# Input projection of a hybrid decoder layer: parts of A's queries and keys written two tiles late, weight loads moved up, inputs kept by token tile, bias rows stored one by one, attention B's loads moved up

## The chip, the cores and the metric

The kernel runs on one core of one Trainium2 chip. The metric is the device time of one execution in microseconds. The core's engines are TensorE (PE), VectorE (DVE), ScalarE (ACT), GpSimd (POOL) and SyncE (SP); each works through its own instructions in order. All data moves between memory and the on-chip buffers through DMA engines that the core's queues share.

## The reference

One decoder layer in float32, 2048 tokens of width 1024. Two head groups, A (sliding window, 8 query heads and 2 key heads, rotary positions) and B (8 heads, three dilated branches with a relative-position bias), read one normalised input through one projection.

```
h = rmsnorm(x, g_attn)
proj = einsum('bsd,de->bse', h, w_in) + b_in        # w_in: 1024 x 2304
qa, ka, va, qb, kb, vb = split(proj)                # 512, 128, 128, 512, 512, 512
oa = sliding_window_sink_gqa(rope(qa), rope(ka), va, sinks)
ob = dilated_mixture(qb, kb, vb, rel_table)         # branches (128,1), (512,4), (2048,16)
mixed = concat(rmsnorm(oa, g_out_a), rmsnorm(ob, g_out_b))
x = x + mixed @ w_o
h = rmsnorm(x, g_ffn)
x = x + (silu(h @ w_gate) * (h @ w_up)) @ w_down
return rmsnorm(x, g_final)
```

## The kernel before

Every float32 operand of a matrix product is kept as two parts, a high part in a reduced format and the rest, and a product is three matmuls: high by high, rest by high, high by rest. The kernel runs in stages: the input is normalised and transposed, and the values of both groups are projected (to about 146 us of the profiled execution); A's keys and queries are projected and rotated (146 to 270); B's queries and keys are projected while A's attention runs (280 to 576); then attention B, the output projection and the feed-forward layer, which takes the second half of the span.

A scheduler in the tile framework sets the order of the instructions on each engine. It takes the program's order and its own estimate of durations; a tile's buffers are taken in turn from a pool with a fixed number of them (`bufs`), and whoever writes into a buffer waits for its last reader.

The names that matter here, all in `project`, `bias_tables` and `attend_b`:

- `hh` and `hl` hold the two parts of the normalised input, 128 partitions by 8 chunks of the width by 2048 tokens. Tokens come in four tiles of 512. `gemm` (L173) makes one output block of 128 columns by one token tile with 24 matmuls into a PSUM buffer `acc`.
- `load_w` (L161 to L165) loads a block of the weights (`raw`) and splits it (`wh` on ScalarE, `wl` on VectorE).
- A's loop goes over the column blocks c = 4 (the keys), 0, 1, 2, 3, and inside over the token tiles. `acc` is copied with its quarters exchanged into `t1` (L298 on ScalarE, L300 on VectorE), multiplied by the rotary tables (L302, L303), summed on GpSimd into `t2` (L304), and split into the two parts of `hia` (the cast L308 on ScalarE, the subtraction L309 on VectorE). `hia` holds all four token tiles of a block and has one buffer. After the fourth tile `store_heads` (L179) writes it to `qA` or `kA` in memory, two DMAs of 1 MB.
- `bias_tables` makes one table per head of B. `rows` multiplies on TensorE (`accb`, L381), copies three rows on ScalarE into `lt` (L382) and stores them to `Ls` (L383). `table` loads pieces of them (L387, L389, L392) into `tt`, `n4` and `n1`, which have one buffer each, rearranges them on VectorE (L393, L394) and stores the table to `Ts` (L396). The steps of the eight heads are laid between the tiles of A's loop.
- `proj_b` makes B's queries and keys, 32 units of one block and token tile, with the parts in `hi` (L331, L332), stored to `qB` and `kB` by `store_heads` on SyncE. `MixerA` (A's attention) runs between the units; its loads of A's keys are at L529.
- `attend_b` loads for each head q (L604), k (L609), the bias table (L612) and v (L621 to L627), all on SyncE. The logits are at L429, the products with v at L494.

Of the kernel before, what the change touches and what calls it, by code (L numbers as in the profile page):

```python
# [10 lines left out]
F32 = mybir.dt.float32  # L11
# [10 lines left out]
NH = 8  # L22
# [125 lines left out]
def project(tc, es, ident, half, x, g_attn, w_in, b_in, sinks, rel, rope, mask_a, onehot, sc):  # L148
# [3 lines left out]
    cp = es.enter_context(tc.tile_pool(name="c1", bufs=1, reuse_waits="tile"))  # L152
    gcol = cp.tile([P, KC], F32, name="gcol")
    bcol = cp.tile([P, 18], F32, name="bcol")
    hh = cp.tile([P, KC, S], F32R, name="hh")
    hl = cp.tile([P, KC, S], F32R, name="hl")
    wr = es.enter_context(tc.tile_pool(name="w1", bufs=2, reuse_waits="tile"))

    def load_w(c0):
# [8 lines left out]
    def gemm(ps, w, t, tag="mm"):  # L168
        acc = ps.tile([P, 512], F32, tag=tag, name="acc")
        n = 0  # L170
        for k in range(KC):
            for a, h in ((w[0], hh), (w[0], hl), (w[1], hh)):
                nc.tensor.matmul(acc, a[:, k, :], h[:, k, t * 512:(t + 1) * 512], start=(n == 0), stop=(n == 3 * KC - 1))  # L173
                n += 1
        return acc

    def store_heads(dst, h, hi, cols):
        for u in range(2):
            nc.sync.dma_start(dst[h + u].rearrange("s d n -> d s n")[:, :, cols], hi[u * 64:u * 64 + 64].bitcast(F32))  # L179


    with ExitStack() as ex:
# [22 lines left out]
        def norm_x(t):  # L205
# [20 lines left out]
            for k in range(KC):  # L226
                pt = ps.tile([P, 512], F32, tag="mm", name="pt")
                for i in range(4):
                    nc.tensor.transpose(pt[:, i * P:(i + 1) * P], ht[i][:, k * P:(k + 1) * P], ident)
                hs = hh[:, k, t * 512:(t + 1) * 512]  # L230
                nc.scalar.activation(hs, pt, AF.Copy, scale=gcol[:, k:k + 1])
                nc.vector.scalar_tensor_tensor(hl[:, k, t * 512:(t + 1) * 512], pt, gcol[:, k:k + 1],
                                               hs.bitcast(F32), op0=ALU.mult, op1=ALU.subtract)

        def v_rows(w, hf, r):
            acc = ps.tile([P, 320], F32, tag="mm", name="accv")
            n = 0
            for k in range(KC):
                for h, b in ((hh, w[0]), (hh, w[1]), (hl, w[0])):
                    nc.tensor.matmul(acc, h[:, k, r * P:(r + 1) * P], b[:, k, :], start=(n == 0), stop=(n == 3 * KC - 1))  # L240
# [35 lines left out]
    with ExitStack() as ex:  # L276
        ps = ex.enter_context(tc.tile_pool(name="ps2", bufs=8, space=PSUM, reuse_waits="tile"))
        rc = ex.enter_context(tc.tile_pool(name="r2", bufs=1, reuse_waits="tile"))
        tab = rc.tile([P, 2, S], F32, name="tab")
        for t in range(NT):  # L280
            cols = slice(t * 512, (t + 1) * 512)
            nc.sync.dma_start(tab[:, :, cols], rope[:, :, cols].rearrange("s p n -> p s n"))
        bsw = rc.tile([P, 5], F32, name="bsw")
        for q4 in range(4):
            nc.vector.tensor_copy(bsw[q4 * 32:(q4 + 1) * 32, :], bcol[(q4 ^ 1) * 32:((q4 ^ 1) + 1) * 32, 0:5])
        bias = bias_tables(tc, ex, ps, rel, onehot, sc)
        rp = ex.enter_context(tc.tile_pool(name="r1", bufs=2, reuse_waits="tile"))
        for n, c in enumerate((4, 0, 1, 2, 3)):
            w = load_w(c * P)
            hi = rp.tile([P, 2, S], F32R, tag="hi", name="hia", bufs=1)  # L290
            for t in range(NT):
                cols = slice(t * 512, (t + 1) * 512)
                acc = gemm(ps, w, t)
                t1 = rp.tile([P, 512], F32, tag="t1", name="t1")
                for q4 in range(4):
                    d, s4 = t1[q4 * 32:(q4 + 1) * 32, :], acc[(q4 ^ 1) * 32:((q4 ^ 1) + 1) * 32, :]
                    if q4 % 2:
                        nc.scalar.copy(d, s4)  # L298
                    else:
                        nc.vector.tensor_copy(d, s4)  # L300
                t2 = rp.tile([P, 512], F32, tag="t2", name="t2")
                nc.vector.scalar_tensor_tensor(t2, acc, bcol[:, c:c + 1], tab[:, 0, cols], op0=ALU.add, op1=ALU.mult)  # L302
                nc.vector.scalar_tensor_tensor(t1, t1, bsw[:, c:c + 1], tab[:, 1, cols], op0=ALU.add, op1=ALU.mult)  # L303
                nc.gpsimd.tensor_add(t2, t2, t1)  # L304

                hj = [hi[:, u].rearrange("p (j r a) -> p r j a", j=16, r=16)[:, 4 * t:4 * t + 4] for u in range(2)]
                t2 = t2.rearrange("p (r j a) -> p r j a", r=4, j=16)
                nc.scalar.copy(hj[0], t2)  # L308
                nc.vector.tensor_sub(hj[1], t2, hj[0].bitcast(F32))  # L309
                if t == NT - 1:  # L310
                    store_heads(sc.qA if c < 4 else sc.kA, 2 * c if c < 4 else 0, hi, slice(0, S))
                m = n * NT + t - 2
                if 0 <= m < 2 * NH:
                    bias(m // NH, m % NH)


    with ExitStack() as ex:
        ps = ex.enter_context(tc.tile_pool(name="ps3", bufs=2, space=PSUM, reuse_waits="tile"))
        ev = ex.enter_context(tc.tile_pool(name="e3", bufs=2, reuse_waits="tile"))
        att = MixerA(tc, ex, ident, sinks, mask_a, sc)  # L320
        w = None

        def proj_b(todo, ps=ps, tag="mm"):
            nonlocal w
            for c0, c, t in todo:
                if t == 0:
                    w = load_w(c0 + c * P)
                bc = bcol[:, c0 // P + c:c0 // P + c + 1]
                acc = gemm(ps, w, t, tag)
                hi = ev.tile([P, 2, 512], F32R, tag="hi", name="hi")  # L330
                nc.scalar.activation(hi[:, 0], acc, AF.Identity, bias=bc)  # L331
                nc.vector.scalar_tensor_tensor(hi[:, 1], acc, bc, hi[:, 0].bitcast(F32), op0=ALU.add, op1=ALU.subtract)  # L332
# [15 lines left out]
def bias_tables(tc, es, ps, rel, onehot, sc):  # L348
# [13 lines left out]
    ones = bp.tile([P, P], F32, name="ones")  # L362
    nc.vector.memset(ones, 1.0)
    for b in range(3):
        o32 = bw.tile([P, 384], F32, tag="lt", name="o32", bufs=1)
        nc.sync.dma_start(o32, onehot[:, b, :])
        nc.vector.tensor_copy(ohr[:, b, :], o32)

# [6 lines left out]
    def rows(h):  # L375
        lw = bw.tile([P, P], F32R, tag="lw", name="lw")
        nc.vector.tensor_scalar(out=lw, in0=ones, scalar1=rhi[:, h:h + 1].bitcast(F32), scalar2=None, op0=ALU.mult)
        lt = bw.tile([P, 3, 384], F32, tag="lt", name="lt", bufs=1)
        for b in range(3):
            acc = ps.tile([P, 384], F32, tag="mm", name="accb")  # L380
            nc.tensor.matmul(acc, lw, ohr[:, b, :], start=True, stop=True)  # L381
            nc.scalar.copy(lt[:, b, :], acc)  # L382
        nc.sync.dma_start(sc.L[h].rearrange("b p n -> p b n"), lt)  # L383

    def table(h):
        tt = bw.tile([P, 640], F32, tag="tt", name="tt", bufs=1)
# [910 lines left out]
```

## Time and profile before

| | us |
|---|---|
| median of three runs | 2429.14 |
| lowest and highest | 2422.71, 2431.72 |
| profiled execution | 2422.51 |
| span of that execution | 2420.7 |
| TensorE busy in it | 2299.3 (95%) |
| VectorE, ScalarE, GpSimd busy | 1602.5, 1055.3, 466.1 |
| mean granted clock of TensorE | 0.975 |

The span is what the profile covers; 1.8 us of the profiled execution lie around it. In a row of the timeline the first number is the start, the second the length, then engine, line, operation and names, with the number of like instructions behind an x; in brackets stands how long the engine had been idle before, and what ended that. PEld is the loading of weights into TensorE. SPq and ACTq are the DMA issues of SyncE and ScalarE.

### The profile page before, as it was taken

What the parts mean: (1) busy time and instruction counts of PE and PEld (TensorE: products, weight loads), DVE (VectorE), ACT (ScalarE), POOL (GpSimd) and SP (SyncE); (2) the same over time, 40 slices, a digit from 0 to 9 for tenths busy, and PEclk for the clock granted to TensorE, in tenths of its full rate; (3) what the DMA queues carried; (4) which work ended last, traced back from release to release, by engine and by line L of the source; (5) the groups of instructions that cost most, each with busy time, mean ns of one, the idle gap of its engine ahead of it and who ended that gap; (6) DMA issues with size and microseconds to landing.
All of it is one profiled execution on the core that took longest, in us unless ns stands there. A gap on an engine that the chain in (4) does not pass through costs nothing.

```text
span 2420.7 us, 33828 instructions
## 1 busy us (share of the span) xinstructions
PE 2299.3 (95%) x11765; PEld 1957.9 (81%) x11765; DVE 1602.5 (66%) x3151; ACT 1055.3 (44%) x2371; POOL 466.1 (19%) x418
## 2 busy tenths in 40 slices
PE   7998889997999989897999999999999999999998
PEld 7987678886999878776788888778888878888887
DVE  5345544446999977658877776796776746657555
ACT  5323245452988873325323323343323325444442
POOL 2321211111111010014132322423232331000000
PEclk9999999998999989998999999999999999999999
DMA  7657575659798686855645445342332329768651
GB/s 222 208 190 196 135 196 164 177 146 248 197 217 216 169 268 175 260 168 183 204 148 173 157 153 170 115 150 96 101 114 94 111 79 396 264 194 292 200 191 70
DMA packets 279835, 436.20 MB, mean 180 GB/s; under 512 B 23968, under 2 KB 152608, under 8 KB 272880
## 3 DMA queue, kind: packets, MB, share of 16 engines
q1 hardware_dynamic: 275648, 423.41, 57.2%
q0 software_dynamic: 3728, 10.30, 1.5%
q8 instruction: 93, 1.52, 0.3%
q14 instruction: 78, 0.64, 0.1%
q10 hardware_dynamic: 288, 0.33, 0.0%
HBM read 286.50 MB, written 147.46 MB: 179 GB/s over the span
## 4 chain that ended last, share of the span: by engine, by line
PE 51%; DVE 3%; DMA 1%; issue 1%; POOL 0%; ACT 0%; DVEq 0%; POOLq 0%; SPq 0%; ACTq 0%
PE bY L1225 7%; PE Yu L1031 7%; PE Yg L1031 7%; PE bZ L1225 5%; PE bX L1225 5%; PE Xu L1031 5%; PE Zu L1031 5%; PE Xg L1031 4%; PE Zg L1031 4%; PE acco L893 2%; DMA hraw<-hT 1%; DMA ob<-oB 1%; DVE xs L915 0%; DVE wl L998 0%; DVE s L979 0%
## 5 line engine op out<-in xcount | busy, mean ns | idle before, releaser
L1178 DVE TENSOR_TENSOR o<-r,o 128x1024 fp32r<-128x1024 f32 x154 | 190.7, 1244 | 139.2 <-ACT o L1177 132.1
L1177 ACT CAST o<-r 128x1024 fp32r<-128x1024 f32 x154 | 162.2, 1054 | 227.4 <-DMA r<-in_w_down_dram 62.6
L1125 POOL TENSOR_TENSOR c<-c,c 128x512 f32<-128x512 f32 x66 | 104.6, 1585 | 569.9 <-DVE c L1049 373.3
L996 ACT CAST wh<-T 128x512 fp32r<-128x512 f32 x176 | 107.4, 621 | 245.0 <-PE Yu L1031 78.8
L476 DVE TENSOR_TENSOR hl<-pt,hl 128x512 fp32r<-128x512 f32 (+1 forms) x224 | 145.7, 658 | 82.5 <-ACT hl L475 81.9
L451 ACT ACTIVATE p<-t,m 128x256 f32<-128x256 f32 (+1 forms) x384 | 176.7, 476 | 20.0 <-DVE m L676 20.0
L173 PE MATMUL acc<-hh,wh 128*128 128x512 f32 x416 | 166.0, 399 | 16.9 <-DVE t L302 9.6
L1225 PE MATMUL bY<-o 128*128 128x512 f32 x792 | 180.5, 389 | 0.0
L1225 PEld LDWEIGHTS bY<-o 128*128 128x128 f32 x792 | 148.6, 188 | 30.9
L893 PE MATMUL acco<-woh,oT 128*128 128x512 f32 x512 | 165.3, 401 | 4.7 <-ACT oT L864 3.9
L173 PE MATMUL acc<-hh,wl 128*128 128x512 f32 x416 | 165.5, 398 | 0.0
L173 PE MATMUL acc<-hl,wh 128*128 128x512 f32 x416 | 165.0, 397 | 0.0
L998 DVE TENSOR_TENSOR wl<-T,wh 128x512 fp32r<-128x512 f32 x176 | 152.7, 879 | 0.3
L494 PE MATMUL o<-hl,v 128*128 128x128 f32 (+1 forms) x816 | 142.8, 296 | 5.9 <-DVE hl L476 4.9
L475 ACT CAST hl<-pt 128x512 fp32r<-128x512 f32 (+1 forms) x224 | 124.7, 566 | 47.9 <-PE pt L470 47.6
L429 PE MATMUL s<-k,q 128*128 128x256 f32 (+1 forms) x768 | 126.2, 299 | 16.5 <-DMA k<-kB 7.9
L470 PE MATMUL pt<-ident,p 128*128 128x128 f32 x848 | 135.8, 282 | 2.5 <-DVE hl L476 1.5
L429 PEld LDWEIGHTS s<-k,q 128*128 128x128 f32 x768 | 105.2, 201 | 24.2 <-DVE nma L566 7.1
L494 PEld LDWEIGHTS o<-hl,v 128*128 128x128 f32 x816 | 113.0, 195 | 11.1 <-DVE hl L476 8.7
L1225 PE MATMUL bX<-o 128*128 128x512 f32 x528 | 120.6, 389 | 1.1 <-DVE o L1178 1.1
L1225 PE MATMUL bZ<-o 128*128 128x512 f32 x528 | 120.3, 389 | 0.0
L893 PEld LDWEIGHTS acco<-woh,oT 128*128 128x128 f32 x512 | 97.9, 192 | 27.3 <-ACT oT L864 4.5
(465 smaller groups left out, 5804.5 us busy)
## 6 DMA issues: line engine op xcount, KB each, us to landing
r<-actS SPq DMA_DIRECT2D x154, 256.0 KB
actS<-c SPq DMA_DIRECT2D x128, 256.0 KB
wraw_g<-in_w_gate_dram SPq DMA_DIRECT2D x44, 512.0 KB
wraw_u<-in_w_up_dram SPq DMA_DIRECT2D x44, 512.0 KB
r<-wT SPq DMA_DIRECT2D x88, 256.0 KB
r<-in_w_down_dram SPq DMA_DIRECT2D x66, 256.0 KB
k<-kB SPq DMA_DIRECT2D x32, 512.0 KB
draw<-in_w_down_dram SPq DMA_DIRECT2D x22, 512.0 KB
```

The source lines that it names most:

```text
L173: nc.tensor.matmul(acc, a[:, k, :], h[:, k, t * 512:(t + 1) * 512], start=(n == 0), stop=(n == 3 * KC - 1))
L429: nc.tensor.matmul(s[:, i, :n], b["q"], b["k"][m], start=(m == 0), stop=(m == 1))
L451: nc.scalar.activation(b["pv"](p[:, i, :n]), b["tv"](b["t"]), AF.Exp, scale=-1.0, bias=nm[:, c:c + 1], accum_out=l[:, c:c + 1])
L470: nc.tensor.transpose(pt[:, sl, :], p[:, i, hfn * P:(hfn + 1) * P], ident)
L476: nc.vector.tensor_sub(lo, pt[:, a:z, :], hi.bitcast(F32))
L494: nc.tensor.matmul(out, v[:, vi, :], mov, start=(first and n == 1), stop=(last and n == 2 * len(jobs)))
L893: nc.tensor.matmul(acc, oT[kk // 2][:, kk % 2, a, i * P:(i + 1) * P], b[:, kk, :], start=(n == 0), stop=(n == 11))
L998: nc.vector.tensor_sub(lo, src, hi.bitcast(F32))
L1031: nc.tensor.matmul(bank, a[:, k], b[:, k], start=(first and m == 0), stop=(m == 11), skip_group_check=not first)
L1177: nc.scalar.copy(o[:, 0], r)
L1178: V.tensor_sub(o[:, 1], r, o[:, 0].bitcast(F32))
L1225: nc.tensor.matmul(bank[i], o[:, u, 0, i * P:(i + 1) * P], o[:, v, 1, :], start=(first and j == 0 and m == 0), stop=(j == NP - 1 and m == ...
```

## The change

Six edits:

1. The inputs `hh` and `hl` become four tiles each, one per token tile.
2. In A's loop, the split of `t2` into `hia` (now the function `parted`) is written two token tiles after the rest of its tile (`rotated`), and `t2` has four buffers instead of two.
3. The weights of A's next column block are loaded at the second token tile of the current one.
4. In `bias_tables` each row has its own `lt` buffer out of two, and its own store: three DMAs of 192 KB per head instead of one of 576 KB.
5. B's last column block of queries and that of keys are made by turns, token tile by token tile, and their stores are issued by ScalarE.
6. With these, the scheduler places other instructions differently, attention B's first loads among them.

```diff
-    hh = cp.tile([P, KC, S], F32R, name="hh")
-    hl = cp.tile([P, KC, S], F32R, name="hl")
+    hh, hl = [], []
+    for t in range(NT):
+        hh.append(cp.tile([P, KC, 512], F32R, name=f"hh{t}"))
+        hl.append(cp.tile([P, KC, 512], F32R, name=f"hl{t}"))
...
-    def store_heads(dst, h, hi, cols):
+    def store_heads(dst, h, hi, cols, q=nc.sync):
         for u in range(2):
-            nc.sync.dma_start(dst[h + u].rearrange("s d n -> d s n")[:, :, cols], hi[u * 64:u * 64 + 64].bitcast(F32))
+            q.dma_start(dst[h + u].rearrange("s d n -> d s n")[:, :, cols], hi[u * 64:u * 64 + 64].bitcast(F32))
...
+        def rotated(c, t, w):
...
+            t2 = rp.tile([P, 512], F32, tag="t2", name="t2", bufs=4)
...
+            return t2.rearrange("p (r j a) -> p r j a", r=4, j=16)
+
+        def parted(c, t, t2):
+
+            if t == 0:
+                his[c] = rp.tile([P, 2, S], F32R, tag="hi", name="hia", bufs=1)
+            hi = his[c]
...
+            nc.scalar.copy(hj[0], t2)
+            nc.vector.tensor_sub(hj[1], t2, hj[0].bitcast(F32))
+            if t == NT - 1:
+                store_heads(sc.qA if c < 4 else sc.kA, 2 * c if c < 4 else 0, hi, slice(0, S))
+
+        his, behind, w = {}, [], {}
+        seq = [(c, t) for c in (4, 0, 1, 2, 3) for t in range(NT)]
+        w[4] = load_w(4 * P)
+        for n, (c, t) in enumerate(seq):
+            t2 = rotated(c, t, w[c])
+            if t == 1 and n + 3 < len(seq):
+                cn = seq[n + 3][0]
+                w[cn] = load_w(cn * P)
+            behind.append((c, t, t2))
+            if len(behind) > 2:
+                parted(*behind.pop(0))
+            if 0 <= n - 2 < 2 * NH:
+                bias((n - 2) // NH, (n - 2) % NH)
+        for x_ in behind:
+            parted(*x_)
...
-                store_heads(sc.kB if c0 == C_KB else sc.qB, 2 * c, hi, slice(t * 512, (t + 1) * 512))
+                store_heads(sc.kB if c0 == C_KB else sc.qB, 2 * c, hi, slice(t * 512, (t + 1) * 512),
+                            nc.scalar if c == 3 else nc.sync)
...
-        units = [(c0, c, t) for c in range(4) for c0 in (C_QB, C_KB) for t in range(NT)]
+        units = [(c0, c, t) for c in range(3) for c0 in (C_QB, C_KB) for t in range(NT)]
+        units += [(c0, 3, t) for t in range(NT) for c0 in (C_QB, C_KB)]
...
-        o32 = bw.tile([P, 384], F32, tag="lt", name="o32", bufs=1)
+        o32 = bw.tile([P, 384], F32, tag="lt", name="o32")
...
-        lt = bw.tile([P, 3, 384], F32, tag="lt", name="lt", bufs=1)
         for b in range(3):
             acc = ps.tile([P, 384], F32, tag="mm", name="accb")
             nc.tensor.matmul(acc, lw, ohr[:, b, :], start=True, stop=True)
-            nc.scalar.copy(lt[:, b, :], acc)
-        nc.sync.dma_start(sc.L[h].rearrange("b p n -> p b n"), lt)
+            lt = bw.tile([P, 384], F32, tag="lt", name="lt")
+            nc.scalar.copy(lt, acc)
+            nc.sync.dma_start(sc.L[h, b], lt)
```

Three places show what this makes of the order. The rows give line, operation, what is written and read, and the shape; a row with an x stands for so many in a run.

ScalarE around the first casts of the second column block (the pair of `hia` that waits for the store of `kA`), before:

```order
61 L298 COPY t_1879<-acc 32x512 x2
62 L308 CAST hia<-t_1835 128x4x16x8
63 L308 CAST hia<-t_1884 128x4x16x8
64 L298 COPY t_1928<-acc 32x512
65 L382 COPY lt<-accb 128x384 x3
66 L298 COPY t_1928<-acc 32x512
67 L163 CAST wh_2208<-raw_2206 128x1024
68 L298 COPY t_1977<-acc 32x512
69 L382 COPY lt<-accb 128x384
70 L308 CAST hia<-t_1933 128x4x16x8
```

The same place now:

```order
63 L297 COPY t_1890<-acc 32x512 x2
64 L312 CAST hia<-t_1842 128x4x16x8
65 L402 COPY lt<-accb 128x384
66 L312 CAST hia<-t_1895 128x4x16x8
67 L402 COPY lt<-accb 128x384
68 L297 COPY t_1951<-acc 32x512
69 L402 COPY lt<-accb 128x384
70 L297 COPY t_1951<-acc 32x512
71 L402 COPY lt<-accb 128x384 x2
72 L165 CAST wh_2122<-raw_2120 128x1024
73 L312 CAST hia<-t_1956 128x4x16x8
```

The casts stand where they stood; the copies of the bias rows are spread singly between them, each with a store of its own behind it.

ScalarE at the end of A's projection (the last column block; t_2444 and t_2492, now t_2475 and t_2523, are its token tiles 0 and 1), before:

```order
100 L298 COPY t_2487<-acc 32x512 x2
101 L308 CAST hia<-t_2444 128x4x16x8
102 L308 CAST hia<-t_2492 128x4x16x8
103 L298 COPY t_2535<-acc 32x512 x2
104 L163 CAST wh_2963<-raw_2961 128x1024
```

And now:

```order
107 L297 COPY t_2518<-acc 32x512 x2
108 L312 CAST hia<-t_2475 128x4x16x8
109 L312 CAST hia<-t_2523 128x4x16x8
110 L297 COPY t_2568<-acc 32x512 x2
111 L165 CAST wh_3001<-raw_2999 128x1024
```

Nothing moved here: both casts still stand ahead of the copies of token tile 2. On SyncE, the store of the third column block and the tables of the last two heads, before:

```order
161 L396 DMA Ts<-tt 128x640
162 L392 DMA n_2502<-Ls 32x1x256 x4
163 L387 DMA tt<-Ls 128x128
164 L396 DMA Ts<-tt 128x640
165 L179 DMA qA<-hia 64x2x2048 x2
166 L537 DMA qa<-qA 128x2x512 x2
```

And now:

```order
177 L416 DMA Ts<-tt 128x640
178 L412 DMA n_2535<-Ls 32x1x256
179 L181 DMA qA<-hia 64x2x2048 x2
180 L407 DMA tt<-Ls 128x128
181 L412 DMA n_2535<-Ls 32x1x256 x2
182 L416 DMA Ts<-tt 128x640
183 L557 DMA qa<-qA 128x2x512 x2
```

The store now stands ahead of the last head's table, of which the remaining loads and the store of `Ts` follow it. SyncE at the start of attention B, before:

```order
242 L179 DMA kB<-hi 64x2x512 x2
243 L533 DMA va<-vA 128x5x128
244 L179 DMA kB<-hi 64x2x512 x2
245 L604 DMA q_5428<-qB 128x2048
246 L609 DMA k_0_5430<-kB 64x2048 x2
247 L609 DMA k_0_5433<-kB 64x2048 x2
248 L612 DMA tab_5436<-Ts 128x640
249 L627 DMA v_2_5438<-vJ 128x16x128
250 L604 DMA q_5446<-qB 128x2048
```

And now:

```order
256 L553 DMA va<-vA 128x5x128
257 L624 DMA q_5466<-qB 128x2048
258 L629 DMA k_0_5468<-kB 64x2048 x2
259 L629 DMA k_0_5471<-kB 64x2048 x2
260 L632 DMA tab_5474<-Ts 128x640
261 L624 DMA q_5484<-qB 128x2048
262 L629 DMA k_1_5486<-kB 64x2048 x2
263 L629 DMA k_1_5489<-kB 64x2048 x2
264 L647 DMA v_2_5476<-vJ 128x16x128
```

The last stores of `kB` have left the queue, and the 1 MB load of v stands behind the loads of the second head.

More of the change, by code (lines that the diff above doesn't have):

```diff
@@ L172, in gemm @@
             for a, h in ((w[0], hh), (w[0], hl), (w[1], hh)):
-                nc.tensor.matmul(acc, a[:, k, :], h[:, k, t * 512:(t + 1) * 512], start=(n == 0), stop=(n == 3 * KC - 1))
+                nc.tensor.matmul(acc, a[:, k, :], h[t][:, k, :], start=(n == 0), stop=(n == 3 * KC - 1))
                 n += 1
         return acc
-    def store_heads(dst, h, hi, cols):
+    def store_heads(dst, h, hi, cols, q=nc.sync):
         for u in range(2):
-            nc.sync.dma_start(dst[h + u].rearrange("s d n -> d s n")[:, :, cols], hi[u * 64:u * 64 + 64].bitcast(F32))
+            q.dma_start(dst[h + u].rearrange("s d n -> d s n")[:, :, cols], hi[u * 64:u * 64 + 64].bitcast(F32))
     with ExitStack() as ex:
@@ L229, in norm_x @@
                     nc.tensor.transpose(pt[:, i * P:(i + 1) * P], ht[i][:, k * P:(k + 1) * P], ident)
-                hs = hh[:, k, t * 512:(t + 1) * 512]
+                hs = hh[t][:, k, :]
                 nc.scalar.activation(hs, pt, AF.Copy, scale=gcol[:, k:k + 1])
-                nc.vector.scalar_tensor_tensor(hl[:, k, t * 512:(t + 1) * 512], pt, gcol[:, k:k + 1],
+                nc.vector.scalar_tensor_tensor(hl[t][:, k, :], pt, gcol[:, k:k + 1],
                                                hs.bitcast(F32), op0=ALU.mult, op1=ALU.subtract)
@@ L239, in v_rows @@
                 for h, b in ((hh, w[0]), (hh, w[1]), (hl, w[0])):
-                    nc.tensor.matmul(acc, h[:, k, r * P:(r + 1) * P], b[:, k, :], start=(n == 0), stop=(n == 3 * KC - 1))
+                    nc.tensor.matmul(acc, h[r // 4][:, k, (r % 4) * P:(r % 4 + 1) * P], b[:, k, :], start=(n == 0), stop=(n == 3 * KC - 1))
                     n += 1
@@ L287, in project @@
         rp = ex.enter_context(tc.tile_pool(name="r1", bufs=2, reuse_waits="tile"))
[L288 to L314, printed above, removed]
@@ new lines, in rotated @@
+        def rotated(c, t, w):
+            cols = slice(t * 512, (t + 1) * 512)
+            acc = gemm(ps, w, t)
+            t1 = rp.tile([P, 512], F32, tag="t1", name="t1")
+            for q4 in range(4):
+                d, s4 = t1[q4 * 32:(q4 + 1) * 32, :], acc[(q4 ^ 1) * 32:((q4 ^ 1) + 1) * 32, :]
+                if q4 % 2:
+                    nc.scalar.copy(d, s4)
+                else:
+                    nc.vector.tensor_copy(d, s4)
+            t2 = rp.tile([P, 512], F32, tag="t2", name="t2", bufs=4)
+            nc.vector.scalar_tensor_tensor(t2, acc, bcol[:, c:c + 1], tab[:, 0, cols], op0=ALU.add, op1=ALU.mult)
+            nc.vector.scalar_tensor_tensor(t1, t1, bsw[:, c:c + 1], tab[:, 1, cols], op0=ALU.add, op1=ALU.mult)
+            nc.gpsimd.tensor_add(t2, t2, t1)
+            return t2.rearrange("p (r j a) -> p r j a", r=4, j=16)
@@ new lines, in parted @@
+        def parted(c, t, t2):
+            if t == 0:
+                his[c] = rp.tile([P, 2, S], F32R, tag="hi", name="hia", bufs=1)
+            hi = his[c]
+            hj = [hi[:, u].rearrange("p (j r a) -> p r j a", j=16, r=16)[:, 4 * t:4 * t + 4] for u in range(2)]
+            nc.scalar.copy(hj[0], t2)
+            nc.vector.tensor_sub(hj[1], t2, hj[0].bitcast(F32))
+            if t == NT - 1:
+                store_heads(sc.qA if c < 4 else sc.kA, 2 * c if c < 4 else 0, hi, slice(0, S))
@@ L320, in project @@
         att = MixerA(tc, ex, ident, sinks, mask_a, sc)
-        w = None
+        w = {}
         def proj_b(todo, ps=ps, tag="mm"):
-            nonlocal w
             for c0, c, t in todo:
                 if t == 0:
-                    w = load_w(c0 + c * P)
+                    w[c0] = load_w(c0 + c * P)
                 bc = bcol[:, c0 // P + c:c0 // P + c + 1]
-                acc = gemm(ps, w, t, tag)
+                acc = gemm(ps, w[c0], t, tag)
                 hi = ev.tile([P, 2, 512], F32R, tag="hi", name="hi")
```

## The prediction

> **What bounds the kernel now.** I read the page's share of busy time first, then TensorE's waits and timeline, then the granted clock by windows, then the engines that feed the places where TensorE stops.
>
> ```profile
> span 2420.7 us, 33828 instructions
> PE 2299.3 (95%) x11765; PEld 1957.9 (81%) x11765; DVE 1602.5 (66%) x3151; ACT 1055.3 (44%) x2371; POOL 466.1 (19%) x418
> ...
> PE s L429 <- DMA ka<-kA: 10.5, 1, 10.5
> PE acc L173 <- DVE t L302: 9.6, 1, 9.6
> PE acc L173 <- ACT lt L382: 6.6, 2, 5.8
> PE accb L381 <- DVE ohr L367: 1.3, 1, 1.3
> ...
> 200.65 0.80 PE L173 MATMUL acc<-hh,wh 128*128 128x512 f32 x1 [5.84 <-ACT lt L382]
> ...
> 279.87 0.80 PE L173 MATMUL acc<-hh,wh 128*128 128x512 f32 x1 [9.59 <-DVE t L302]
> ...
> 314.09 1.83 PE L429 MATMUL s<-ka,qa 128*128 128x128 f32 x7 [10.52 <-DMA ka<-kA]
> ...
> 569.89 0.77 PE L429 MATMUL s<-k,q 128*128 128x128 f32 x2 [6.96 <-DMA k<-kB]
> ...
> 574.25 0.96 PE L429 MATMUL s<-k,q 128*128 128x128 f32 x6 [0.90 <-DMA k<-kB]
> ```
>
> TensorE is busy for 95% of the span: it is idle for 2420.7 - 2299.3 = 121 us in all. The four rows of waits are all that it waited for between 160 and 320 us (columns: us in total, times, longest). With the two rows at attention B's start they come to 10.5 + 9.6 + 6.6 + 1.3 + 7.0 + 0.9 = 36 us. None is for a weight tile. After a long stop the clock is down as well:
>
> ```profile
> 200.00:204.00 4.00, 3.35 (x8) 0.50 0.46 154
> ...
> 312.00:316.00 4.00, 1.91 (x8) 0.50 0.99 332
> ...
> 500.00:545.00 45.00, 45.00 (x269) 1.00 0.59 158
> ...
> 574.00:578.00 4.00, 2.92 (x21) 1.00 1.18 336
> ```
>
> The columns are the window, its length, TensorE's busy time and matmuls, the granted clock, the DMA share and GB/s. Right after the stops the clock is 0.50, for some 4 us, so each long stop costs about 2 us more. Four of them: 8 us. The most that this change can win is therefore about 36 + 8 = 44 us, 1.8%.
>
> What holds TensorE at 200, 280 and 314 us is the evacuation of A's projection. One buffer hia holds the parts of all four token tiles, and the next column block's first cast waits until it has been stored:
>
> ```profile
> 195.87 1.14 ACT L308 CAST hia<-t 128x512 fp32r<-128x512 f32 x2 [7.12 <-DMA kA<-hia]
> ...
> 228.37 1.15 ACT L308 CAST hia<-t 128x512 fp32r<-128x512 f32 x2 [7.20 <-DMA qA<-hia]
> ...
> 261.50 1.14 ACT L308 CAST hia<-t 128x512 fp32r<-128x512 f32 x2 [7.91 <-DMA qA<-hia]
> ...
> 286.70 1.14 ACT L308 CAST hia<-t 128x512 fp32r<-128x512 f32 x2 [7.66 <-DMA qA<-hia]
> ```
>
> From cast to cast the loop takes 32.5, 33.1 and 25.2 us. The 7.9 us longer rounds are those that also carry the bias tables. TensorE would need less, and by 270 us it has filled PSUM and stops. So a change in this stage is worth what it takes out of that loop, once: the end of the stage is the load of A's keys at 314 us, queued behind the last store of the loop.
>
> **The change part by part.**
>
> Parts two tiles late, four buffers of t2. In the program they come later, but on ScalarE the built order is the same row for row from the middle of the third column block on: the casts of tiles 0 and 1 of the last block still stand ahead of the copies of its tile 2, and still wait for the store of the block before. ScalarE works in order, so the 7.66 us wait stays and so do the copies behind it. VectorE's rows there are the same too, and its subtraction precedes the next use of a t2 buffer, so two more buffers free nothing. I count 0. Bounds: nothing lost, as no instruction is added; the gain, were the order to be overcome, is the first rival.
>
> Weights early: 0, as no row above waits for a weight; what hides them is the 24 matmuls of each tile. The same for the inputs by token tile: no instruction more or less.
>
> Bias rows in three stores with a ring of two. Eight stores become 24. A copy now waits until the store two before it has landed. Rows for it:
>
> ```profile
> 166.15 0.38 SPq L383 DMA_DIRECT2D Ls<-lt  x1
> 169.19 0.33 SPq L387 DMA_DIRECT2D tt<-Ls  x1
> ...
> 209.39 0.43 SPq L383 DMA_DIRECT2D Ls<-lt  x1
> ...
> 215.05 1.25 ACT L382 COPY lt<-accb 128x384 f32<-128x384 f32 x3 [1.91 <-DMA Ls<-lt]
> ...
> 212.52 0.62 ACT L308 CAST hia<-t 128x512 fp32r<-128x512 f32 x1
> ...
> 215.61 1.27 SPq L179 DMA_DIRECT2D qA<-hia  x2
> ```
>
> A store of 576 KB landed 169.19 - 166.53 = 2.66 us after its issue with free DMA engines, and 215.05 - 209.82 = 5.23 us with loaded ones. A third of it moves 384 KB less, which at the 332 GB/s of the window above is 1.2 us, so it lands in 1.5 to 4.0 us (an estimate). I take 2.3, nearer to the free case, as the DMA share after 200 us is 0.46. Between the casts at 195.87 and the cast of tile 3, ten copies stand on ScalarE. Two of them per round of copy 0.42 (1.25 / 3), issue 0.43 and landing 2.3 are 1.6 us a copy, 16 us in all; before it was 212.52 - 195.87 = 16.65. So I take -0.8 us, with ends of -3 (then TensorE is behind) and +8 (landing 4.0). SP's 16 more issues of some 0.4 us cost 6.5 us of a queue that stands empty between rows; part of this is inside that end.
>
> The next round changes more, because on SyncE the last head's table store now stands behind the store of qA instead of ahead of it, and on VectorE that head's copies behind the subtraction that this store needs:
>
> ```profile
> 238.06 0.39 DVE L393 COPY tt<-n 128x256 f32<-128x256 f32 x1 [2.37 <-DMA Ts<-tt]
> ...
> 246.19 0.39 DVE L393 COPY tt<-n 128x256 f32<-128x256 f32 x1 [2.69 <-DMA Ts<-tt]
> 247.57 0.40 DVE L394 COPY tt<-n 128x256 f32<-128x256 f32 x1 [0.99 <-DMA n<-Ls]
> ...
> 248.72 0.69 DVE L309 TENSOR_TENSOR hia<-t,hia 128x512 fp32r<-128x512 f32 x1
> ...
> 249.44 0.63 SPq L179 DMA_DIRECT2D qA<-hia  x1
> ```
>
> The rows at 246.19 and 247.57 leave that path: 2.69 + 0.39 + 0.99 + 0.40 = 4.5 us. The heads ahead of it run half a head later than before, by which I take 1.1 off: -3.4 (ends -4.5 and +3, one more wait like the 2.69). What is late next is that last head: its loads queue behind the 2 MB store, and VectorE's copy (0.40) with a rest of the wait stands ahead of the next block's subtractions: +1.0.
>
> Attention B's first loads, and stores on ScalarE's queue:
>
> ```profile
> 554.33 0.74 DVE L332 SCALAR_TENSOR_TENSOR hi<-acc,bcol,hi 128x512 fp32r<-128x512 f32 x1
> ...
> 555.10 1.23 SPq L179 DMA_DIRECT2D kB<-hi  x2
> 556.42 0.64 SPq L604 DMA_DIRECT2D q<-qB  x1
> 557.11 3.76 SPq L609 DMA_DIRECT2D k<-kB  x4
> ...
> 1.20 0.45 ACTq L269 DMA_DIRECT2D brow<-in_b_in_dram  x1
> ...
> 613.55 0.39 PE L494 MATMUL o<-hl,v 128*128 128x256 f32 x1
> ```
>
> In the changed order q's first load still waits for the last projection's evacuation (554.33), since it lands where the bias column lies. Only the two kB stores, 1.23 us, no longer stand ahead of it. Their 512 KB still share the engines with q and k, and the first logits now stand 18 rows earlier on TensorE, with output matmuls of A behind them that used to run ahead of the wait. They then run after it, where the 0.90 us wait is. I take -0.7 (ends -2 and +2). The large v load moves behind the second head's q and k; it is first read at 613.55, 57 us later, so 0. The 16 stores cost ScalarE 16 x 0.45 = 7 us of issuing plus a wait for VectorE each, spread over the last eight projection tiles. ScalarE is busy for 44% of the span, and TensorE, which is busy for 45.00 of 45.00 us there, covers it: 0, and if the cover fails, 2 us.
>
> A page would have it otherwise only in one reading. The row says that the stores leave SyncE; one could hope that a second queue also carries them beside the loads, and with 512 KB at 332 GB/s that would be 1.6 us more. The Trainium skill, "DMA: Bandwidth & Descriptors", section "Issuing engines are not separate DMA queues", says that transfers started by different engines run on the same 16 DMA engines and interleave; by that rule the sum keeps its -0.7, by the hope it is -2.3. No run so far shows which.
>
> Sum: -0.8 - 3.4 + 1.0 - 0.7 = -3.9 us. The profiled execution took 2422.51 us (2420.7 of span and 1.8 around it), which gives 2418.6. The median of the three runs is 2429.14, 6.6 above that execution, so against the median I forecast 2425.
>
> **The rivals.**
>
> The late parts do what they say. If the copies of tiles 2 and 3 got past the waiting casts, the loop would lose most of its 7.12 + 7.20 + 7.91 + 7.66 = 29.9 us of waiting, and TensorE's stops at 200, 280 and 314 us (26 us) would shrink to the 4 or so that the loads of A's keys need, with two slow-clock stretches less: 2429 - 26 = 2403. For it speaks the size of the stops, against it the unchanged order on ScalarE. 8%.
>
> The tables run much faster. A head's loads begin before its third row is stored.
>
> ```profile
> DVE tt L393 <- DMA Ts<-tt: 8.7, 4, 2.7
> ...
> DVE tt L394 <- DMA n<-Ls: 4.1, 5, 1.1
> ```
>
> If these waits of VectorE all left the loop, it would end 12.8 us sooner, and with one slow-clock stretch of 2 us less the time is 2429 - 15 = 2414. Against it: each head's table still waits for the store of the one before, as the 2.37 and 2.69 show. 19%.
>
> Slower: the ring of two. Each copy waits for a landing, and on SyncE the small stores stand behind table loads that themselves wait. If a store of 192 KB takes the whole 5.23 us, ten copies cost 10 x (5.23 - 2.3) / 2 = 14.7 us more than I took; the loop then ends 10.8 us later than before, and with two more stops long enough for the slow clock (4 us) the time is 2429 + 15 = 2444. From a landing of about 4.7 us on this decides. 16%.
>
> On that clock: the rows show 0.50 after stops of 5.84 us and more, and 1.00 after the one of 0.90 us. The Trainium skill, "TensorE: Matmul & The Clock Gate", Part 1, has the clock fall to half after an idle window of some 3.4 us. By that rule stops of 2 to 3 us, as a ring would make, cost nothing more, and this rival would end at 2440 instead of 2444. The rows agree so far as they go.
>
> The change does nothing that can be measured: loop and loads stay as they are, 2429. 15%.
>
> **How the numbers follow.** My forecast, from about 10 us faster to a few slower, has 42%. A measurement of this kernel tells about 0.5%, 12 us, from no change: the three runs lie 9 us apart. Faster by more than that are the first two rivals, 27%; slower the third, 16%; the rest, 57%, is within. The range reaches below to just above the first rival, 2404, and above to the third, 2444; each leaves out about a tenth.
>
> **What would show it.** Right: on ScalarE the four casts that wait 7 to 8 us for a store of hia are still there; the stops before the evacuation of the last block and for A's keys remain, at 9 and 10 us, a few us earlier; the second qA store of the projection is issued some 20 us or less after the cast that began its round, down from 21; the first k of attention B comes one us sooner. Wrong: long waits of lt copies for Ls stores (over 8 us in total by much), new stops of TensorE on lt between 165 and 230 us, or the stop at 280 us gone.

## The result and the profile after

The changed kernel took 2415.69 us in the median of six runs (2412.19 to 2418.66), the kernel before 2429.79 beside it: a ratio of 0.9946 with a 95% interval of 0.9929 to 0.9963. A second comparison later gave 2417.34 against 2426.92, 0.9963 (0.9948 to 0.9979). It is 10 to 14 us faster. Both intervals leave out 1, though the gain is no more than about the 12 us that the prediction took for the least that can be told from no change. I forecast 2425 and a sum of 3.9 us. The time lies inside the range of 2404 to 2444, but that is luck: the gain comes from the start of attention B, to which I gave 0.7 us, and from the output projection, which no term of mine holds, and the bias rows, which I counted as a gain, are a loss that takes back a part of it.

The page of the changed kernel (the profiled execution took 2418.66 us):

```profile
span 2416.9 us, 33849 instructions
PE 2295.9 (95%) x11765; PEld 1953.6 (81%) x11765; DVE 1601.3 (66%) x3151; ACT 1056.2 (44%) x2371; POOL 466.5 (19%) x418
```

TensorE's waits between 160 and 320 us, and its timeline at the stops that the prediction spoke of (idle time and what ended it in brackets):

```profile
PE acc L175 <- DVE t L301: 13.7, 2, 10.0
PE accb L400 <- ACT lt L402: 6.5, 3, 2.5
PE s L449 <- DMA ka<-kA: 4.6, 1, 4.6
```

```profile
284.39 0.80 PE L175 MATMUL acc<-hh,wh 128*128 128x512 f32 x1 [10.04 <-DVE t L301]
...
318.65 1.35 PE L449 MATMUL s<-ka,qa 128*128 128x128 f32 x7 [4.60 <-DMA ka<-kA]
...
575.08 1.62 PE L449 MATMUL s<-k,q 128*128 128x128 f32 x6 [0.56 <-DMA k<-kB]
```

A's loop still stops TensorE at the same places, later than before (284 for 280, 319 for 314 us). The stop of 6.96 us for the first k of attention B is gone. ScalarE's timeline shows why the loop is later:

```profile
174.53 0.48 ACT L402 COPY lt<-accb 128x384 f32<-128x384 f32 x1 [2.84 <-DMA Ls<-lt]
...
185.82 0.48 ACT L402 COPY lt<-accb 128x384 f32<-128x384 f32 x1 [5.50 <-DMA Ls<-lt]
...
200.60 0.62 ACT L312 CAST hia<-t 128x512 fp32r<-128x512 f32 x1 [6.76 <-DMA kA<-hia]
...
234.87 1.15 ACT L312 CAST hia<-t 128x512 fp32r<-128x512 f32 x2 [6.29 <-DMA qA<-hia]
...
265.40 1.14 ACT L312 CAST hia<-t 128x512 fp32r<-128x512 f32 x2 [6.66 <-DMA qA<-hia]
...
291.27 1.14 ACT L312 CAST hia<-t 128x512 fp32r<-128x512 f32 x2 [7.71 <-DMA qA<-hia]
```

The four casts wait for the stores as before. The copies of the bias rows now wait for their own stores ahead of the first cast, which comes at 200.60 instead of 195.87 us. Long waits of these copies were the first sign of being wrong that the prediction named.

To see where the time went I cut every profiled execution at four instructions that each kernel has: the long row of A's logits that waits for its keys (314.09 before), the first matmul of the output projection (889.02), the first of the feed-forward layer (1117.00) and the first of its second part (1992.84). The first column counts from the start of the span, each of the others from the instruction before. There is one execution for each row, so a difference of 1 or 2 us says little:

| kernel | up to A's long row | to the output projection | output projection | feed-forward, first part | rest | span |
|---|---|---|---|---|---|---|
| before | 314.1 | 574.9 | 228.0 | 875.8 | 427.9 | 2420.7 |
| changed | 318.6 | 570.6 | 224.5 | 875.3 | 427.9 | 2416.9 |
| changed, second comparison | 317.6 | 567.7 | 222.2 | 875.7 | 428.8 | 2411.9 |
| e1_units | 313.3 | 570.1 | 222.4 | 874.9 | 428.8 | 2409.6 |
| e2_nobias | 314.1 | 568.0 | 223.6 | 875.5 | 427.8 | 2409.0 |
| e11_ring3 | 313.6 | 569.4 | 222.5 | 875.3 | 427.8 | 2408.7 |
| e6_actq | 317.1 | 572.7 | 223.0 | 875.4 | 427.8 | 2416.0 |
| e3_bias | 317.6 | 575.6 | 229.9 | 875.9 | 427.9 | 2426.9 |
| e4_nounits | 317.2 | 575.5 | 229.2 | 874.8 | 427.9 | 2424.6 |
| e5_turns | 313.5 | 578.8 | 228.8 | 875.6 | 427.8 | 2424.5 |
| e7_act1 | 316.0 | 574.7 | 229.0 | 875.7 | 428.8 | 2424.2 |
| e8_late | 311.8 | 574.1 | 226.8 | 875.6 | 428.8 | 2417.1 |
| e9_kb8 | 314.9 | 570.9 | 227.4 | 882.2 | 427.8 | 2423.3 |
| e10_act15 | 314.1 | 576.3 | 227.9 | 876.2 | 427.9 | 2422.4 |

The six rows with all sixteen stores on ScalarE (the changed kernel twice, e1, e2, e11 and e6) lie at 567.7 to 572.7 and 222.2 to 224.5 in the second and third stretch; of the others none is below 570.9 and 226.8. The whole gain lies in these two stretches, some 6 us (mean 569.7 against 575.8 for before, e3, e4, e5 and e8) and 5 us (223.0 against 228.4 for all eight others), less what A's loop loses.

### The profile page after: what moved, and what is told of

Same layout as the page of the kernel before. It is cut to its first block, busy times and chain, and to the rows that moved or that the text cites. A ratio compares the mean times of both kernels' runs of the same rounds, so it can differ in the third digit from the quotient of the medians.

```text
span 2416.9 us, 33849 instructions
## 1 busy us (share of the span) xinstructions
PE 2295.9 (95%) x11765; PEld 1953.6 (81%) x11765; DVE 1601.3 (66%) x3151; ACT 1056.2 (44%) x2371; POOL 466.5 (19%) x418
## 4 chain that ended last, share of the span: by engine, by line
PE 51%; DVE 5%; DMA 3%; issue 1%; POOL 0%; ACT 0%; DVEq 0%; POOLq 0%; SPq 0%; ACTq 0%
PE bY L1245 7%; PE Yu L1051 7%; PE Yg L1051 6%; PE bZ L1245 5%; PE bX L1245 5%; PE Zu L1051 4%; PE Xu L1051 4%; PE Xg L1051 4%; PE Zg L1051 4%; PE acco L913 3%; DMA ob<-oB 1%; DVE wl L1018 1%; DMA ob<-oA 1%; DVE xs L935 1%; DMA hraw<-hT 0%
## 5 line engine op out<-in xcount | busy, mean ns | idle before, releaser
L1145 POOL TENSOR_TENSOR c<-c,c 128x512 f32<-128x512 f32 x66 | 104.3, 1580 | 570.1 <-DVE c L1069 390.7
L1245 PEld LDWEIGHTS bX<-o 128*128 128x128 f32 x528 | 99.0, 188 | 22.1 <-DVE o L1198 1.5
```

The lines of the kernel that those rows point to most:

```text
L1245: nc.tensor.matmul(bank[i], o[:, u, 0, i * P:(i + 1) * P], o[:, v, 1, :], start=(first and j == 0 and m == 0), stop=(j == NP - 1 and m == ...
```

## The experiments

Ratios are to the kernel before on the same chip, with 95% intervals.

**Which part.** e1: the kernel before with the part on B's last column block alone, both the turns and ScalarE's stores:

```diff
+                store_heads(..., nc.scalar if c == 3 else nc.sync)
...
-        units = [(c0, c, t) for c in range(4) for c0 in (C_QB, C_KB) for t in range(NT)]
+        units = [(c0, c, t) for c in range(3) for c0 in (C_QB, C_KB) for t in range(NT)]
+        units += [(c0, 3, t) for t in range(NT) for c0 in (C_QB, C_KB)]
```

> The kernel before with the last part alone: B's last block of queries and keys by turns, their stores issued by ScalarE. Theory 1 (the gain comes from the start of attention B, and the bias rows' ring costs some 5 us in A's loop): TensorE's stop of 7 us before the first k of attention B is gone or under 2 us, the clock after it stays at 1.00, A's loop is as before (casts of hia at 196, 228, 262, 287 us), and the time is 10 to 19 us below the kernel before, ratio 0.992 to 0.996. Theory 2 (the gain comes from the bias rows, in executions less lucky than the profiled one): within 5 us of the kernel before, ratio 0.998 to 1.001. Theory 3 (the gain comes from the inputs kept by token tile or from where the tiles lie): within 3 us.

Measured: 2411.94 us, 0.9938 (0.9926 to 0.9951). This part alone gives all of the gain.

e2: the changed kernel with the bias rows as before (one `lt` of three rows, one store):

```diff
+        lt = bw.tile([P, 3, 384], F32, tag="lt", name="lt", bufs=1)
...
-            lt = bw.tile([P, 384], F32, tag="lt", name="lt")
-            nc.scalar.copy(lt, acc)
-            nc.sync.dma_start(sc.L[h, b], lt)
+            nc.scalar.copy(lt[:, b, :], acc)
+        nc.sync.dma_start(sc.L[h].rearrange("b p n -> p b n"), lt)
```

> The changed kernel with the bias rows as before: one buffer, one store of 576 KB a head. Theory 1: A's loop gets back its 4.6 us, so 3 to 8 us faster than the changed kernel's ratio of 0.9946, ratio 0.991 to 0.994; A's loop ends (first matmul on A's keys) at 312 to 315 us instead of 318.7. Theory 2: the gain goes, ratio 0.998 to 1.001. Theory 3: as the changed kernel, 0.993 to 0.996.

Measured: 2410.74 us, 0.9933 (0.9919 to 0.9947). Against e1 this kernel also has the late parts, the early weights and the inputs by token tile; the two differ by 1.2 us, inside both intervals.

e3: the kernel before with the bias part alone (the diff of e2 the other way round).

> The kernel before with the bias rows' part alone: two buffers, three stores a head. Theory 1: A's loop ends 3 to 6 us later, TensorE's stop at attention B's start stays at 6 to 8 us, ratio 1.001 to 1.003. Theory 2: ratio 0.993 to 0.996. Theory 3: ratio 0.999 to 1.002.

Measured: 2429.21 us, 1.0015 (1.0002 to 1.0028): a small loss.

e4: the changed kernel without the part on B's last block (the diff of e1 the other way round).

> The changed kernel with B's last block in the old order and its stores on SyncE. Theory 1: the stop at attention B's start is back (5 to 8 us and the slow clock behind it), ratio 0.999 to 1.003. Theory 2: ratio 0.993 to 0.996, as the changed kernel. Theory 3: ratio 0.993 to 0.997.

Measured: 2427.49 us, 1.0015 (0.9999 to 1.0030). Without that part the change gains nothing.

e8: the kernel before with the late parts, four buffers of `t2` and the early weights alone:

```diff
+            t2 = rp.tile([P, 512], F32, tag="t2", name="t2", bufs=4)
...
+            if t == 1 and n + 3 < len(seq):
+                cn = seq[n + 3][0]
+                w[cn] = load_w(cn * P)
+            behind.append((c, t, t2))
+            if len(behind) > 2:
+                parted(*behind.pop(0))
```

> The kernel before with the parts of A's queries and keys two tiles late, four buffers of t2 and the early weights alone. My prediction's step: nothing, ratio 0.9985 to 1.0015, first long row on A's keys at 312 to 316 us. Rival: the stop before it shrinks and the loop ends sooner, ratio 0.990 to 0.997.

Measured: 2423.23 us, 0.9995 (0.9983 to 1.0007). ScalarE's timeline has three of the four casts waiting as before; the second waits 4.37 instead of 7.20 us:

```profile
196.35 1.14 ACT L310 CAST hia<-t 128x512 fp32r<-128x512 f32 x2 [7.16 <-DMA kA<-hia]
...
232.71 1.14 ACT L310 CAST hia<-t 128x512 fp32r<-128x512 f32 x2 [4.37 <-DMA qA<-hia]
...
258.53 1.15 ACT L310 CAST hia<-t 128x512 fp32r<-128x512 f32 x2 [7.36 <-DMA qA<-hia]
...
284.31 1.14 ACT L310 CAST hia<-t 128x512 fp32r<-128x512 f32 x2 [7.50 <-DMA qA<-hia]
```

**Turns, stores or order.** e5: the kernel before with the turns alone, all stores on SyncE (`units` as in e1, no `nc.scalar`).

> The kernel before with B's last block of queries and keys made by turns, all stores still issued by SyncE. In the built order attention B's start and the output projection stand as before. Theory A (the stores on ScalarE's queue make the gain, half of it at attention B's start, half in the output projection, whose order they change): within 4 us of the kernel before, ratio 0.9985 to 1.0015, first k of attention B some 256 us after the first long row on A's keys, output projection 229 us. Theory B (the turns bring attention B's first k forward): ratio 0.993 to 0.996.

Measured: 2425.55 us, 1.0002 (0.9989 to 1.0014).

e6: the kernel before with ScalarE's 16 stores alone, `units` unchanged:

```diff
-                store_heads(sc.kB if c0 == C_KB else sc.qB, 2 * c, hi, slice(t * 512, (t + 1) * 512))
+                store_heads(sc.kB if c0 == C_KB else sc.qB, 2 * c, hi, slice(t * 512, (t + 1) * 512),
+                            nc.scalar if c == 3 else nc.sync)
```

> The kernel before with the last column block's 16 stores issued by ScalarE, the units in the old order. The built order has both the changed start of attention B and the changed output projection. Theory A: ratio 0.992 to 0.996, the stage from A's keys to the output projection some 570 us instead of 575, output projection some 223 us instead of 229. Theory B: ratio 0.998 to 1.001.

Measured: 2413.93 us, 0.9947 (0.9933 to 0.9961). So of the edits it is the move of the sixteen stores that gains, and the turns give nothing. As the order of attention B changes with the move, this alone does not tell the queue from the order.

e7: only the last two stores of `kB` on ScalarE, those that stand ahead of attention B's first q:

```diff
+                            nc.scalar if c == 3 and c0 == C_KB and t == NT - 1 else nc.sync)
```

> The kernel before with the last unit's two kB stores alone issued by ScalarE. In the built order attention B's start is the changed one, the output projection's order is that of the kernel before. Theory A: only the first half of the gain, ratio 0.996 to 0.9985, the stage from A's keys to the output projection some 570 us, output projection 228 to 230 us. Theory C (all of the gain is attention B's start, and the output projection's 5 us are chance): ratio 0.9925 to 0.9955.

Measured: 2424.22 us, 0.9996 (0.9986 to 1.0006). Its SyncE starts attention B much as the changed kernel's does, but TensorE's rows there are ordered in a third way, and the output projection stands as before. The table has no gain in either stretch. Cut once more, at the first matmul of B's logits, a part of it is there: from A's long row to this matmul it is 251.9 us in e7, 251.3 to 253.3 in e9 and the six kernels with all sixteen stores moved, and 255.8 to 257.8 in the six others. In its execution e7 loses this again at once: from there to the first product with v it takes 45.4 us at a granted clock of 0.73, where the kernel before takes 43.7 at 0.80.

From the first of B's logits on, e1, e2, e6, e11 and the changed kernel have the same order on TensorE and SyncE; e3, e4, e5 and e8 have that of before. The difference reaches far behind the stores: in the output projection, more than 300 us later, VectorE's rows are ordered anew. VectorE after the first `ms_o` there, before:

```
L116 TENSOR_SCALAR ms_o_10354<-pss 128x4
L856 TENSOR_TENSOR ob<-ob 128x512
L903 SCALAR_TENSOR_TENSOR xs_10285<-acco,rs_o_10356,xs_10285 128x512 x3
L858 TENSOR_TENSOR os__10434<-ob,fb 128x512
```

And in the changed kernel:

```
L116 TENSOR_SCALAR ms_o_10392<-pss 128x4
L923 SCALAR_TENSOR_TENSOR xs_10323<-acco,rs_o_10394,xs_10323 128x512 x3
L876 TENSOR_TENSOR ob<-ob 128x512
L923 SCALAR_TENSOR_TENSOR xs_10323<-acco,rs_o_10394,xs_10323 128x512
```

No line of the diff names these rows. SyncE's rows differ there too (the loads of x stand ahead of the stores of `hT`), and a few of TensorE's and ScalarE's. The next two kernels are chosen by their built order, to have one of the two places without the other.

e9: only the eight stores of the last kB block on ScalarE. Attention B then starts nearly as in the changed kernel, and SyncE in the output projection stands as before:

```diff
+                            nc.scalar if c == 3 and c0 == C_KB else nc.sync)
```

> The kernel before, with the eight stores of the last kB block alone issued by ScalarE (those of the last qB block stay on SyncE). In its built order attention B starts nearly as in the changed kernel (no kB store and no 1 MB load of v ahead of the first q and k), while SyncE in the output projection stands row for row as before. Theory of two places: the gain of ScalarE's stores is about 5 us up to the first k of attention B and about 5 us in the output projection, each by its own order. Then the stretch from the last long row of A's logits to the first output-projection matmul is some 570 us (before 575), the output projection some 228 us (as before), and the time 2421 (ratio 0.998). Rival, ScalarE's queue itself or the start of attention B carries all: 2414 (0.995), with an output projection of 223 us. If neither: 2426 (1.000).

Measured: 2426.54 us, 1.0011 (0.9999 to 1.0023). The two stretches came as the theory of two places said, 570.9 and 227.4 us; the time did not. TensorE in the first part of the feed-forward layer, in e9 and in the changed kernel (window, length, busy time and matmuls, clock, DMA share, GB/s):

```profile
1113.29:1995.46 882.17, 855.98 (x3696) 0.99 0.41 137
```

```profile
1113.68:1988.99 875.31, 854.94 (x3696) 0.99 0.40 135
```

It is idle there for 882.17 - 855.98 = 26.2 us instead of 20.4, which takes back what attention B gave. In e9 the built order of this layer is another one again.

e10: all but the last kB unit's two stores on ScalarE, so fourteen of sixteen. One kB store and the 1 MB load of v stay ahead, as before; SyncE's rows in the output projection are those of the changed kernel:

```diff
+                            nc.scalar if c == 3 and (c0 == C_QB or t < 3) else nc.sync)
```

> The kernel before, with ScalarE issuing all 16 stores but the two of the last kB unit. In its built order one kB store stands right ahead of the first q, and the 1 MB load of v ahead of the second head's q, as before; SyncE in the output projection stands as in the changed kernel (x loads ahead of the stores of hT). Theory of two places: the output projection takes some 223 us (before 228), the stretch up to it about 575 us as before, and the time is 2421 (ratio 0.998). Rival, the start of attention B carries all and the output projection only follows: 228 us there and 2426 (1.000). Rival, ScalarE's queue itself whatever the order: 2414 (0.995).

Measured: 2429.41 us, 1.0014 (0.9999 to 1.0029). Up to the output projection it takes 576.3 us, as expected; the output projection takes 227.9, against expectation. So neither fourteen stores on ScalarE's queue nor SyncE's order in the output projection is enough for the gain there. VectorE's order differs in e10: it starts as the one shown of before. The output projection in before, changed kernel, e6 and e10:

```profile
889.02:1117.00 227.98, 206.84 (x960) 0.95 0.69 212
```

```profile
889.21:1113.68 224.47, 204.34 (x961) 0.96 0.69 216
```

```profile
889.77:1112.72 222.95, 206.02 (x960) 0.95 0.70 217
```

```profile
890.41:1118.32 227.91, 205.10 (x961) 0.96 0.68 212
```

TensorE's idle time (length less busy) is 21.1, 20.1, 16.9 and 22.8 us; its long waits there are all for VectorE (`xs`, `ms_f`). All six executions with the changed kernel's VectorE order take 222 to 224.5 us and the eight others 227 to 230. TensorE's and ScalarE's orders go with it in the same six, and none of them was tried by itself, since the scheduler sets them: VectorE's fits best, as the waits are for it, but it is not shown.

**The ring.** e11: the changed kernel with a ring of three row buffers (shared, as before, with the start-up tile `o32`), which fits where the one buffer of three rows was:

```diff
-        o32 = bw.tile([P, 384], F32, tag="lt", name="o32")
+        o32 = bw.tile([P, 384], F32, tag="lt", name="o32", bufs=3)
...
-            lt = bw.tile([P, 384], F32, tag="lt", name="lt")
+            lt = bw.tile([P, 384], F32, tag="lt", name="lt", bufs=3)
```

> The changed kernel with a ring of three bias-row buffers instead of two, still with one store per row (24 stores); from attention B on the built order is the same. Theory: the cost of the bias part is the copy that waits for the store two rows before. Then the copies' waits for Ls (2.84 and 5.50 us before the first cast) go, the first cast of the second column block comes some 4 us sooner, and the time is about 2411 (ratio 0.9935), as with the old bias rows. Rival: the 16 more issues on SyncE and the smaller stores themselves cost it; then the time stays at 2415 (0.995).

Measured: 2410.84 us, 0.9946 (0.9932 to 0.9960), with 2424.09 before. The time is that of e2 on the same chip (2410.74). ScalarE's waits for `Ls` between 160 and 300 us in the changed kernel and in e11 (total, times, longest; in the kernel before it is 8.0 us, four times), and the first cast in e11:

```profile
ACT lt L402 <- DMA Ls<-lt: 23.5, 11, 5.5
```

```profile
ACT lt L402 <- DMA Ls<-lt: 2.7, 2, 2.5
```

```profile
197.14 1.14 ACT L312 CAST hia<-t 128x512 fp32r<-128x512 f32 x2 [9.48 <-DMA kA<-hia]
```

e12: the changed kernel again, as its ratio and that of e11 were the same while the times differ by 5 us.

> The changed kernel once more, unedited, with as many rounds as the experiments had, since the ring of three gave 2410.8 in another comparison than the 2415.7 of the changed kernel. Theory, the ring of two costs the changed kernel some 4 us: about 2415 again, the first cast of the second column block again near 200.6 us (197.1 with the ring of three) and the long row of A's logits near 318 (313.6). Rival, the 4.9 us lay between the comparisons: about 2411, with the same late casts made up for elsewhere.

Measured: 2417.34 us, 0.9963 (0.9948 to 0.9979). A's loop ends late again; the long row of A's logits in e12 and in e11:

```profile
317.60 1.83 PE L449 MATMUL s<-ka,qa 128*128 128x128 f32 x7 [4.65 <-DMA ka<-kA]
```

```profile
313.62 1.83 PE L449 MATMUL s<-ka,qa 128*128 128x128 f32 x7 [11.66 <-DMA ka<-kA]
```

So the ring of two costs the loop some 4 us, and a third buffer brings it back with all 24 stores kept. What counts is where the copies wait: in e2 they wait 13.3 us in all, but nowhere ahead of the last cast of the keys, which the store of kA needs; in the changed kernel both waits shown above stand ahead of that cast, at 186.19, and the store is issued at 187.62 instead of 182.96 us. Counted from the first matmul of A's loop, the four executions with the ring of two (changed twice, e3, e4) reach this row after 169.6 to 172.0 us and the ten others after 165.2 to 168.5. e11 and e2 have the shortest times of all, 5 to 7 us below the changed kernel's two; but these were taken in different comparisons, and the ratios, whose intervals overlap, do not set them apart.

## Why the prediction was right or wrong

- **Late parts, 0: right.** e8 is 0.9995, and three of the four casts wait as they did. Early weights are in e8 too, and cost or gain nothing that can be measured. The inputs by token tile were not run alone; e2 and e1 differ by 1.2 us, and their intervals are some 3 us to each side.
- **Bias rows, -0.8 - 3.4 + 1.0 = -3.2: wrong in sign.** The loop came 3.5 to 4.6 us later (317.6 and 318.6 against 314.1). By rounds: from cast to cast 34.3, 30.5 and 25.9 us against 32.5, 33.1 and 25.2, so +1.8, -2.6 and +0.7 where I had -0.8, -3.4 and +1.0. Their sum is -0.1 where I had -3.2; the part of the first that I priced, from the first cast to that of tile 3, is 19.0 us where I had 16 and the kernel before has 16.65. The larger miss is where the account begins: at the cast at 195.87. Ahead of it stand the copies of the first three heads, with the same ring, and there they wait 2.84 + 5.50 us and less in others; with that the first cast comes 4.7 us later, which no term holds. A landing of 2.3 us (from the end of a store's issue to the start of what waits for it) was also too short. SyncE's issues of the third and the sixth store, and of the store of qA below:

```profile
169.60 0.37 SPq L403 DMA_DIRECT2D Ls<-lt  x1
...
180.40 0.42 SPq L403 DMA_DIRECT2D Ls<-lt  x1
...
253.24 1.27 SPq L181 DMA_DIRECT2D qA<-hia  x2
```

  The copy at 174.53, two rows behind the third, starts 4.6 us after its issue ends, and the copy at 185.82 5.0 us after that of the sixth. That is the rival of the ring of two at about its point of decision. It did not cost the 15 us of that rival. A part of the copies' waits falls into time in which the cast would wait for kA's store anyway: 9.48 us in e11, 6.76 in the changed kernel.
- **The second qA store: right.** It is issued at 253.24, 18.4 us after its round's cast at 234.87; I said 20 or less, for 21 before. It did not come earlier in time, as the whole loop is late.
- **Attention B's start, -0.7: mis-sized, about -6.** I priced SyncE's 1.23 us and left the 6.96 us stop for k where it was. TensorE's waits from 540 to 640 us, before and in the changed kernel:

```profile
PE s L429 <- DMA k<-kB: 7.9, 2, 7.0
```

```profile
PE s L449 <- DVE nma L453: 3.4, 1, 3.4
...
PE oa L514 <- ACT p L471: 1.5, 1, 1.5
...
PE s L449 <- DMA k<-kB: 0.6, 1, 0.6
```

  The one long stop is now several short ones, at A's last rows and at k. The first of B's logits comes 251.6 us after A's long row, instead of 255.8: 4 us sooner, where I had said one. The whole stretch from A's long row to the output projection, before and in the changed kernel's second execution (e12), has the same number of matmuls:

```profile
314.09:889.02 574.93, 545.44 (x3764) 0.96 0.74 194
```

```profile
317.60:885.26 567.66, 539.69 (x3764) 0.98 0.76 197
```

  In the means, of the six executions with all sixteen stores moved and of before, e3, e4, e5 and e8, about half of the 6 us is idle time (28.8 instead of 31.6) and half is busy time for the same matmuls (541.0 instead of 544.2), at a granted clock of 0.97 instead of 0.96; single executions of the two groups overlap in both. TensorE in four windows of 20 us, before and in e12:

```profile
554.00:574.00 20.00, 11.41 (x74) 0.83 0.88 240
574.00:594.00 20.00, 17.03 (x98) 0.83 1.08 295
594.00:614.00 20.00, 17.98 (x103) 0.83 1.03 227
614.00:634.00 20.00, 19.91 (x160) 0.91 0.51 142
```

```profile
554.00:574.00 20.00, 15.12 (x96) 0.83 0.86 275
574.00:594.00 20.00, 16.29 (x111) 1.00 1.08 289
594.00:614.00 20.00, 17.63 (x129) 1.00 1.09 220
614.00:634.00 20.00, 19.23 (x167) 1.00 0.76 195
```

  The granted clock is 0.83 to 0.91 in all four windows before and 1.00 in three of four in e12, which gets through 503 matmuls in the 80 us against 435 (not all of one size). The clock differs from execution to execution, and the gain with it: the changed kernel's first profile has 0.86, 0.80, 1.00 and 1.00 and takes 570.6 us for the stretch, against 567.7 in e12; e6, with the same order, has 0.71 in the third window and the smallest gain of the group (572.7). That the shorter stops are what keeps the clock up is not shown.
- **Stores on ScalarE, 0: right as a cost, and no sign that the queue itself gains** (e10, with fourteen of the sixteen, though in an order of its own). The Trainium skill, "DMA: Bandwidth & Descriptors", section "Issuing engines are not separate DMA queues", says that another issuing engine saves the issuing alone. e10, at 1.0014, agrees with that as far as it goes.
- **What no term held:** the output projection, about -5. I compared the built orders at A's loop and at attention B's start, and took the rest for unchanged because the diff names nothing there.
- **The rivals.** That the late parts work is refuted by e8 (2403 foreseen; a ratio of 0.9995 found), that the tables run faster by the later loop. "Nothing" was near for the edits apart from the stores and the ring. My sum was -3.9, against -14.1 and -9.6 measured in the two comparisons: by the stretches, a loss of some 4 where I had a gain of 3, and a gain of some 11 where I had 0.7.

## What to carry to other kernels

Where a scheduler builds the order, moving a few stores to another queue can reorder an engine hundreds of microseconds later; compare the built orders to the end of the kernel, not only around the edit, and measure stretch by stretch, as e9 shows, where one place gives some 4 us and another takes 6. With a ring of fewer buffers than the rows that one step writes, a copy can wait for a landing: start its account at the first copy, look for the wait that holds up a store which others need, and price a landing under the load it will see. A stop of TensorE is priced by its idle time and by the clock after it.

## What was not expected of the hardware

The clock also fell where TensorE had not stopped. Before, in windows of 4 us:

```profile
584.00:588.00 4.00, 3.34 (x20) 0.88 1.02 247
588.00:592.00 4.00, 3.94 (x19) 0.50 1.08 273
592.00:596.00 4.00, 3.93 (x19) 0.50 1.21 243
596.00:600.00 4.00, 3.78 (x16) 0.50 1.21 216
```

The prediction counted some 4 us of slow clock behind each stop. Here it is 0.50 for some 12 us, with the longest stop in the 7 us ahead at 0.67 us and TensorE busy for three quarters or more of each window since 580. The Trainium skill, "TensorE: Matmul & The Clock Gate", Part 1, has the clock fall after an idle window of some 3.4 us; the stop of 6.96 us at 563 to 570 is one, but nothing like it lies ahead of 588, so that rule alone does not give this dip. In e11 the clock is at full speed at the same time; it falls later and for less long, to 0.88 from 596 us and 0.69 from 600, and is at 1.00 again from 604:

```profile
588.00:592.00 4.00, 3.43 (x24) 1.00 1.17 287
592.00:596.00 4.00, 3.44 (x22) 1.00 1.26 186
```

What sets it off stays open.
